# Normalised activations ahead of the first FFN part and the second input projection; convolution taps read from PSUM

## The chip, the cores and the metric

The kernel runs on one core of a Trainium2 chip. The time is device microseconds of one execution. TensorE (PE) multiplies, VectorE (DVE), ScalarE (ACT) and GpSimd (POOL) do element-wise work, SyncE (SP) issues the DMAs.

## The reference

One inference step of a one-layer hybrid decoder: 1024 prompt tokens and 8 sample tokens, model width 1024, FFN width 2816, all float32.

```python
h = rmsnorm(x, norm_mix)                       # x * rsqrt(mean(x*x)+eps) * g
proj = h @ w_in
...                                            # four recurrent mixers: S5, mLSTM, GLA, RWKV-7
x = x + mix @ w_out
h2 = rmsnorm(x, norm_ffn)
ug, uv = split(h2 @ ffn_w_up)                  # gate and value, 2816 columns each
padded = concatenate([ffn_buf, ug])
conv = ffn_conv_b
for j in range(3): conv = conv + ffn_conv_w[j] * padded[:, j:j+T]
x = x + (gelu(conv) * uv) @ ffn_w_down
y = rmsnorm(x, norm_final)
```

## The kernel before

Activations lie with features on the partitions and tokens along the free axis. The tokens are worked on in two segments: 512 prompt tokens, and 520 (the other 512 and the 8 sample tokens). The program is: input projection of segment 0 (`win(0)`), a list of mixer steps (`SEQ0`), input projection of segment 1 (`win(1)`), output projection and FFN of segment 0 (the "first FFN part"), a second list of mixer steps (`SEQ1`: gla, mlstm, rwkv and s5 on the later tokens, then the decode steps of the sample tokens), then output projection and FFN of segment 1 (the "last FFN part"). A list scheduler writes the order of each engine from priorities: weight loads ('S') come first; projections, FFN and mixers are interleaved; the matmuls of `mm3` ('G') have the lowest priority and fill what the mixers leave of PE.

Each float32 product is made of three fp32r matmuls (`mm3`, L1129 to L1131): high part of the weight by high and low part of the activation, low part of the weight by high part of the activation. `load_w` fetches a weight tile (512 KB), casts it on ScalarE (L1111) and forms the low part on GpSimd (L1112, four pieces). `split_gain` (L1181, L1182) multiplies an activation by the norm's gain and splits it, on ScalarE and VectorE. The eight pieces of a segment are the tiles h0 to h7.

The factor rsqrt(mean(x*x)+eps) depends only on the token. It is applied after the matmul. `Ms` collects the squares (L1153, L1154), and `rstd` adds them over the partitions with a matmul by ones (L1161) and makes the factor with Ln and Exp on ScalarE (L1165, L1166). `w_in_fm` multiplies by it when it takes a result out of PSUM (L1204); `w_in_tm`, whose results have tokens on the partitions, uses a copy of the factor with tokens on the partitions that `tokens` makes (L1173 to L1176). The factor of segment 1 (`x_rstd`, k.r1) is computed among the mixer steps of `SEQ0`.

The FFN runs over 22 blocks j of 128 columns. For each block of the first part: 24 matmuls of 512 columns give the gate in a PSUM tile g, 24 more the value. VectorE takes the gate out with the factor (L1302) and the value too (L1309), makes the first tap with bias (L1311) and adds the two others (L1314, L1315), each from the gate in SBUF. GpSimd sets the two columns ahead of the gate to zero (L1312), keeps the last two for the next segment in `halo` (L1319) and multiplies the convolution by the value (L1327). `gelu_gate` (L124 to L126, and L119 to L121 in `sigmoid_`) makes gelu's gate; L1329 multiplies, and `split_act` (L1120, L1121) splits the result into a tile p0 to p4. After every fourth block `down` multiplies four of them by the down weights, and L1290 adds to the residual x2 (tiles xa0 to xa7 for segment 0). PSUM has three tiles g for all this until the last FFN part, which has five more.

The mixers' own PE work is of many small matmuls between VectorE steps. In `rwkv`, L242 and L243 are 31 dependent pairs of VectorE instructions (a triangular solve), L253 the matmuls behind them, and L277 to L297 a chain over four chunks of 64 tokens.

Of the kernel before, what the change touches and what calls it, by code (L numbers as in the profile page):

```python
# [1178 lines left out]
def split_gain(k,N,i,x,gname):  # L1179
# [2 lines left out]
    k.nc.vector.scalar_tensor_tensor(out=h[:,1,0:N],in0=x,scalar=g,in1=h[:,0,0:N].bitcast(F32),op0=ALU.mult,op1=ALU.subtract)  # L1182
    return h

def x_rstd(k,c0,c1):
    N=c1-c0; m=Ms(k,N,1,"mc",1)
# [4 lines left out]
    m.tokens()
    return m

def w_in_fm(k,hr,seg,idx,w=None,tag=None):
# [8 lines left out]
    for (a,b),p in zip(chunks(N),ps):
        nc.vector.scalar_tensor_tensor(out=e[:,a:b],in0=p[:,0:b-a],scalar=sc,in1=r[:,a:b],op0=ALU.mult,op1=ALU.mult)  # L1204
# [69 lines left out]

def ffn(k,c0,c1,x2,rs,last=False,then=None):
    nc=k.nc; V=nc.vector; A=nc.scalar; GP=nc.gpsimd; N=c1-c0
    lastseg=c1==1032; NP=N-8 if lastseg else N
    hs=[split_gain(k,N,i,x2[i][:,0:N],'nffn') for i in range(8)]; ms=None if last else Ms(k,N)
    ch=chunks(N); o=2*last
    hid={}  # L1280
    def down(n):
        ph=[hid.pop(j) for j in range(max(4*n-o,0),min(4*n-o+4,22))]; end=n==5; nm=8//len(ph)
        wd=lambda i,tags=None: load_w(k,(k.wdn,k.wdl)[last][max(4*n-o,0)+i].rearrange("p (m k c)->p m k c",m=nm,c=128),tags)
        if last and end: return ffn_last(k,c0,x2,ch,ph,[wd(0),wd(1),wd(2,("h0","h1")),wd(3,("h2","h3"))])
        for m in range(8):
            if m%nm==0: w=wd(m//nm)
            for a,b in ch:
                p=gps(k)
                mm3(k,p[:,0:b-a],(w[0][:,m%nm],w[1][:,m%nm]),ph,a,b)
                V.tensor_tensor(out=x2[m][:,a:b],in0=x2[m][:,a:b],in1=p[:,0:b-a],op=ALU.add)  # L1290
            if end: ms.add(x2[m][:,0:N])

    for j in range(22):
        wg=load_w(k,k.wup[j,0]); wv=load_w(k,k.wup[j,1])
        g=k.tp.tile([128,HW+2],F32,tag="t",name="t",bufs=k.tb); acc=tt(k)
        pv=[]; pg=[]
        for a,b in ch:
            p=gps(k); pg.append(p)
            mm3(k,p[:,0:b-a],wg,hs,a,b)
        r=rs.rstd()  # L1300
        for (a,b),p in zip(ch,pg):
            V.tensor_tensor(out=g[:,2+a:2+b],in0=p[:,0:b-a],in1=r[:,a:b],op=ALU.mult)  # L1302
        for a,b in ch:
            q=gps(k)
            mm3(k,q[:,0:b-a],wv,hs,a,b)
            pv.append(q)
        if not last:
            qr=tt(k)
            for (a,b),q in zip(ch,pv): V.tensor_tensor(out=qr[:,a:b],in0=q[:,0:b-a],in1=r[:,a:b],op=ALU.mult)  # L1309
        if last: A.activation(out=acc[:,0:N],in_=g[:,2:2+N],func=AF.Identity,scale=v1(k,'cw2',j),bias=v1(k,'cb',j))  # L1310
        else: V.tensor_scalar(out=acc[:,0:N],in0=g[:,2:2+N],scalar1=v1(k,'cw2',j),scalar2=v1(k,'cb',j),op0=ALU.mult,op1=ALU.add)  # L1311
# [2 lines left out]
        V.scalar_tensor_tensor(out=acc[:,0:NP],in0=g[:,1:1+NP],scalar=v1(k,'cw1',j),in1=acc[:,0:NP],op0=ALU.mult,op1=ALU.add)  # L1314
        V.scalar_tensor_tensor(out=acc[:,0:NP],in0=g[:,0:NP],scalar=v1(k,'cw0',j),in1=acc[:,0:NP],op0=ALU.mult,op1=ALU.add)  # L1315
        if lastseg:
            V.tensor_tensor(out=acc[:,NP:N],in0=acc[:,NP:N],in1=k.sdec[:,j],op=ALU.add)
            GP.tensor_copy(k.fcd[:,j],g[:,2+NP:2+N])
        GP.tensor_copy(k.halo[:,j],g[:,NP:NP+2])  # L1319
        if last:  # L1320
            A.activation(out=acc[:,0:N],in_=acc[:,0:N],func=AF.Gelu_apprx_tanh)
            if j==21: k.tc.keep_in_program_order(A.preload_act_table_set("natural_log_exp_and_others"))
            GP.tensor_tensor(out=acc[:,0:N],in0=acc[:,0:N],in1=r[:,0:N],op=ALU.mult)
            for (a,b),q in zip(ch,pv):
                V.tensor_tensor(out=acc[:,a:b],in0=acc[:,a:b],in1=q[:,0:b-a],op=ALU.mult)
        else:
            GP.tensor_tensor(out=qr[:,0:N],in0=acc[:,0:N],in1=qr[:,0:N],op=ALU.mult)  # L1327
            gelu_gate(k,g[:,2:2+N],acc[:,0:N])
            V.tensor_tensor(out=acc[:,0:N],in0=qr[:,0:N],in1=g[:,2:2+N],op=ALU.mult)  # L1329
# [212 lines left out]
```

## Time and profile before

| | us |
|---|---|
| runs shown, median of 3 | 1537.26 (1534.96 to 1538.24) |
| the profiled execution, its own time | 1529.54 |
| its span, first to last instruction | 1527.7 |
| PE busy | 1426.4 (93%) |
| PE weight loads | 1244.7 (81%) |
| VectorE busy | 1055.3 (69%) |
| ScalarE busy | 631.8 (41%) |
| GpSimd busy | 926.5 (61%) |

The page also cuts the span into 40 slices of 38 us. A digit is the busy share in tenths; PEclk is the clock that PE was granted, in tenths of full speed.

```profile
PE   8699999997998989999789999989999999999997
DVE  8998856888588968897896868586436434343444
PEclk9889999998999999999989999999999999999999
```

The last FFN part fills the last ten slices, where PE has no gap and VectorE is a third to a half busy. A matmul is pipelined: its own time (0.40 us for 512 columns) is longer than the distance between two of them (0.23 us), so PE's busy time is read as the union of intervals.

### The profile page before, as it was taken

To read this page: it belongs to the slowest core of one execution; us is meant where nothing else is said; L and a number is where in the kernel's file an instruction comes from. 1 tells how busy PE (TensorE), PEld (TensorE's weight loads), DVE (VectorE), ACT (ScalarE), POOL (GpSimd) and SP (SyncE) were. 2 spreads that over 40 slices of the span, in tenths; PEclk is the share of its full clock that TensorE was granted. 3 is DMA by queue.
4 is the path that set the end of the run, shared out by engine and by line. 5 is a ranking of instruction groups with operands and counts; after the bars stand their busy time and mean duration, and the time that the engine had idled before them with its cause. 6 is when DMAs were issued, how large, how long until landed. Compare 5 with 4: busy or idle time off the path is not lost.

```text
span 1527.7 us, 26826 instructions
## 1 busy us (share of the span) xinstructions
PE 1426.4 (93%) x10123; PEld 1244.7 (81%) x10123; DVE 1055.3 (69%) x2096; ACT 631.8 (41%) x1007; POOL 926.5 (61%) x1182
## 2 busy tenths in 40 slices
PE   8699999997998989999789999989999999999997
PEld 7577779877898767767567777767999999999997
DVE  8998856888588968897896868586436434343444
ACT  6135354534445454463435524334442323232323
POOL 8555354544345455556655567596877758576764
PEclk9889999998999999999989999999999999999999
DMA  6554348434243523532323343324334323223332
GB/s 222 161 161 160 96 150 238 143 93 91 85 145 118 170 84 97 169 111 72 90 67 95 91 149 116 97 89 160 118 105 138 98 85 96 96 87 95 93 91 84
DMA packets 110806, 179.80 MB, mean 118 GB/s; under 512 B 33556, under 2 KB 67732, under 8 KB 110676
## 3 DMA queue, kind: packets, MB, share of 16 engines
q1 hardware_dynamic: 110676, 178.08, 38.2%
q8 instruction: 80, 1.31, 0.4%
q14 instruction: 50, 0.41, 0.1%
HBM read 148.10 MB, written 28.41 MB: 116 GB/s over the span
## 4 chain that ended last, share of the span: by engine, by line
PE 42%; DVE 15%; POOL 3%; ACT 2%; issue 2%; DMA 2%; DVEq 0%; SPq 0%; ACTq 0%; POOLq 0%
PE g L1129 13%; PE g L1130 13%; PE g L1131 13%; POOL wl L1112 2%; DVE r_rs L243 2%; DVE r L242 1%; DVE t L1315 1%; DVE t L1314 1%; DVE t L125 1%; DVE p L1121 1%; DVE xa L1290 0%; DVE t L1372 0%; DVE t L1329 0%; DVE t L126 0%; DMA r<-DB 0%
## 5 line engine op out<-in xcount | busy, mean ns | idle before, releaser
L1112 POOL TENSOR_TENSOR wl<-wr,wh 128x256 fp32r<-128x256 f32 x708 | 593.2, 869 | 242.3 <-ACT wh L1111 220.7
L1131 PE MATMUL g<-h,wl 128*128 128x260 f32 (+1 forms) x1536 | 492.2, 321 | 3.6 <-POOL wl L1112 3.5
L1129 PE MATMUL g<-h,wh 128*128 128x260 f32 (+1 forms) x1536 | 491.9, 321 | 3.0 <-DVE t L1204 1.8
L1130 PE MATMUL g<-h,wh 128*128 128x260 f32 (+1 forms) x1536 | 492.3, 321 | 1.6 <-DVE h L1182 1.4
L1131 PEld LDWEIGHTS g<-h,wl 128*128 128x128 f32 x1536 | 290.1, 189 | 28.5 <-POOL wl L1112 5.9
L1130 PEld LDWEIGHTS g<-h,wh 128*128 128x128 f32 x1536 | 289.5, 189 | 26.9 <-DVE h L1182 2.9
L1129 PEld LDWEIGHTS g<-h,wh 128*128 128x128 f32 x1536 | 289.5, 189 | 25.8 <-issue 2.0
L1111 ACT CAST wh<-wr 128x1024 fp32r<-128x1024 f32 x177 | 185.0, 1045 | 298.8 <-PE g L1130 166.4
L1129 PE MATMUL g<-p,wh 128*128 128x260 f32 (+1 forms) x496 | 162.8, 330 | 17.8 <-DVE xa L1290 6.9
L1130 PE MATMUL g<-p,wh 128*128 128x260 f32 (+1 forms) x496 | 163.0, 329 | 1.4 <-DVE p L1121 1.3
L1131 PE MATMUL g<-p,wl 128*128 128x260 f32 (+1 forms) x496 | 162.8, 329 | 1.3 <-POOL wl L1112 1.3
L1129 PEld LDWEIGHTS g<-p,wh 128*128 128x128 f32 x496 | 94.8, 192 | 28.2 <-DVE xa L1290 7.4
L1131 PEld LDWEIGHTS g<-p,wl 128*128 128x128 f32 x496 | 94.9, 192 | 10.1 <-POOL wl L1112 2.0
L1130 PEld LDWEIGHTS g<-p,wh 128*128 128x128 f32 x496 | 94.6, 191 | 10.3 <-DVE p L1121 2.7
L1112 POOL TENSOR_TENSOR p<-p,p 128x256 fp32r<-128x256 f32 x76 | 62.7, 856 | 54.7 <-ACT p L1111 42.1
L1302 DVE TENSOR_TENSOR t<-g,r 128x260 f32<-128x260 f32 (+1 forms) x66 | 33.6, 511 | 63.6 <-PE g L1131 57.6
L1290 DVE TENSOR_TENSOR xb<-xb,g 128x260 f32<-128x260 f32 x80 | 33.6, 424 | 59.2 <-PE g L1131 59.1
L1314 DVE SCALAR_TENSOR_TENSOR t<-t,vec 128x512 f32<-128x512 f32 x44 | 41.2, 937 | 25.9 <-ACT t L1310 25.3
L1121 DVE TENSOR_TENSOR p<-t,p 128x512 fp32r<-128x512 f32 (+1 forms) x44 | 40.8, 928 | 18.6 <-ACT p L1120 18.4
L1130 PE MATMUL g<-h,p 128*128 128x260 f32 (+1 forms) x144 | 50.8, 353 | 2.1 <-DVE h L1121 2.1
L1129 PE MATMUL g<-h,p 128*128 128x260 f32 (+1 forms) x144 | 51.6, 358 | 0.0
L1131 PE MATMUL g<-h,p 128*128 128x260 f32 (+1 forms) x144 | 50.4, 350 | 0.0
(722 smaller groups left out, 2744.4 us busy)
## 6 DMA issues: line engine op xcount, KB each, us to landing
wr<-in_wup_dram SPq DMA_DIRECT2D x88, 512.0 KB
wr<-in_wfm_dram SPq DMA_DIRECT2D x27, 512.0 KB
wr<-in_wdn_dram SPq DMA_DIRECT2D x22, 512.0 KB
wr<-in_wdl_dram SPq DMA_DIRECT2D x22, 512.0 KB
wr<-in_wout_dram SPq DMA_DIRECT2D x13, 512.0 KB
p<-in_wfm_dram SPq DMA_DIRECT2D x11, 512.0 KB
t<-in_xT_dram SPq DMA_DIRECT2D x16, 260.0 KB
b4c<-B8Td SPq DMA_DIRECT2D x6, 512.0 KB
```

The source lines that it names most:

```text
L125: k.nc.vector.scalar_tensor_tensor(out=t,in0=t,scalar=1.0,in1=x,op0=ALU.add,op1=ALU.mult)
L242: V.tensor_tensor(out=tv,in0=bc(Ls[:,jj+1:32,jj:jj+1],[128,n,m]),in1=bc(X[:,jj:jj+1,0:m],[128,n,m]),op=ALU.mult)
L243: V.tensor_tensor(out=X[:,jj+1:32,0:m],in0=X[:,jj+1:32,0:m],in1=tv,op=ALU.subtract)
L1111: nc.scalar.copy(h[:,0:n],r[:,0:n])
L1112: for c in range(0,n,256): nc.gpsimd.tensor_tensor(out=l[:,c:c+256],in0=r[:,c:c+256],in1=h[:,c:c+256].bitcast(F32),op=ALU.subtract)
L1121: k.nc.vector.tensor_tensor(out=h[:,1,0:N],in0=src,in1=h[:,0,0:N].bitcast(F32),op=ALU.subtract)
L1129: T.matmul(out,wh[:,i],a,start=i==0,stop=False)
L1130: T.matmul(out,wh[:,i],b,start=False,stop=False)
L1131: T.matmul(out,wl[:,i],a,start=False,stop=i==n-1)
L1290: V.tensor_tensor(out=x2[m][:,a:b],in0=x2[m][:,a:b],in1=p[:,0:b-a],op=ALU.add)
L1302: V.tensor_tensor(out=g[:,2+a:2+b],in0=p[:,0:b-a],in1=r[:,a:b],op=ALU.mult)
L1314: V.scalar_tensor_tensor(out=acc[:,0:NP],in0=g[:,1:1+NP],scalar=v1(k,'cw1',j),in1=acc[:,0:NP],op0=ALU.mult,op1=ALU.add)
```

## The change

In `win(1)` and in the first FFN part the factor is now applied to the activations ahead of the split: the new `split_norm` multiplies each of the eight tiles by it on GpSimd and hands the product to `split_gain`. The factor after the matmul goes in these two places. The evictions of `w_in_fm` in `win(1)` become ScalarE activations; `w_in_tm` multiplies by 1.0; `w_in_g` drops its product; `x_rstd` no longer makes the copy with tokens on the partitions. `win(0)` and the last FFN part keep the factor where it was.

In the first FFN part (`gate_first`) the gate stays in PSUM: ScalarE makes the first tap with bias from it, the two other taps read it there and write from column 1 and column 2 on, so that no columns need to be set to zero. ScalarE copies the last two columns into `halo` and takes the value out of PSUM. The last FFN part (`gate_last`) has the same instructions as before.

```diff
+def split_norm(k,N,i,x,r,gname):
+    t=tt(k)[:,0:N]; k.nc.gpsimd.tensor_tensor(out=t,in0=x,in1=r[:,0:N],op=ALU.mult)
+    return split_gain(k,N,i,t,gname)
+
 def x_rstd(k,c0,c1):
...
-    m.tokens()
+    m.rstd()
     return m
 def w_in_fm(k,hr,seg,idx,w=None,tag=None):
...
-    r=r.rstd()
+    if r is not None: r=r.rstd()
     for (a,b),p in zip(chunks(N),ps):
-        nc.vector.scalar_tensor_tensor(out=e[:,a:b],in0=p[:,0:b-a],scalar=sc,in1=r[:,a:b],op0=ALU.mult,op1=ALU.mult)
+        if r is None: nc.scalar.activation(out=e[:,a:b],in_=p[:,0:b-a],func=AF.Identity,scale=sc)
+        else: nc.vector.scalar_tensor_tensor(out=e[:,a:b],in0=p[:,0:b-a],scalar=sc,in1=r[:,a:b],op0=ALU.mult,op1=ALU.mult)
...
 def ffn(k,c0,c1,x2,rs,last=False,then=None):
...
-    hs=[split_gain(k,N,i,x2[i][:,0:N],'nffn') for i in range(8)]; ms=None if last else Ms(k,N)
+    hs=[split_gain(k,N,i,x2[i][:,0:N],'nffn') if last else split_norm(k,N,i,x2[i][:,0:N],rs.rstd(),'nffn') for i in range(8)]; ms=None if last else Ms(k,N)
...
+    def gate_first(j,wg,wv):
+        acc=tt(k); t=tt(k); qr=tt(k); p=up(wg)[0]
+        A.activation(out=acc[:,0:N],in_=p[:,0:N],func=AF.Identity,scale=v1(k,'cw2',j),bias=v1(k,'cb',j))
+        for o,n in ((1,'cw1'),(2,'cw0')): V.scalar_tensor_tensor(out=acc[:,o:N],in0=p[:,0:N-o],scalar=v1(k,n,j),in1=acc[:,o:N],op0=ALU.mult,op1=ALU.add)
+        A.copy(k.halo[:,j],p[:,N-2:N])
+        q=up(wv)[0]
+        A.copy(qr[:,0:N],q[:,0:N])
+        GP.tensor_tensor(out=qr[:,0:N],in0=acc[:,0:N],in1=qr[:,0:N],op=ALU.mult)
+        gelu_gate(k,t[:,0:N],acc[:,0:N])
+        V.tensor_tensor(out=acc[:,0:N],in0=qr[:,0:N],in1=t[:,0:N],op=ALU.mult)
+        return acc
...
-        r=rs.rstd()
-        for (a,b),p in zip(ch,pg):
-            V.tensor_tensor(out=g[:,2+a:2+b],in0=p[:,0:b-a],in1=r[:,a:b],op=ALU.mult)
...
-        if not last:
-            qr=tt(k)
-            for (a,b),q in zip(ch,pv): V.tensor_tensor(out=qr[:,a:b],in0=q[:,0:b-a],in1=r[:,a:b],op=ALU.mult)
-        if last: A.activation(out=acc[:,0:N],in_=g[:,2:2+N],func=AF.Identity,scale=v1(k,'cw2',j),bias=v1(k,'cb',j))
-        else: V.tensor_scalar(out=acc[:,0:N],in0=g[:,2:2+N],scalar1=v1(k,'cw2',j),scalar2=v1(k,'cb',j),op0=ALU.mult,op1=ALU.add)
-        if c0==0: GP.memset(g[:,0:2],0.0)
-        else: GP.tensor_copy(g[:,0:2],k.halo[:,j])
-        V.scalar_tensor_tensor(out=acc[:,0:NP],in0=g[:,1:1+NP],scalar=v1(k,'cw1',j),in1=acc[:,0:NP],op0=ALU.mult,op1=ALU.add)
-        V.scalar_tensor_tensor(out=acc[:,0:NP],in0=g[:,0:NP],scalar=v1(k,'cw0',j),in1=acc[:,0:NP],op0=ALU.mult,op1=ALU.add)
...
     for j in range(22):
         wg=load_w(k,k.wup[j,0]); wv=load_w(k,k.wup[j,1])
+        acc=(gate_last if last else gate_first)(j,wg,wv)
...
     def setup():
...
-                w=[]; hr=[split_gain(k,c1-c0,i,load_x(k,i,c0,c1),'nmix') for i in range(8)],k.r1
+                w=[]; hr=[split_norm(k,c1-c0,i,load_x(k,i,c0,c1),k.r1.rstd(),'nmix') for i in range(8)],None
```

The scheduler writes a new order for all engines from about the middle of `SEQ0` up to the second output projection. Three places follow. In rows of the order, a name is the output tile, then the inputs behind the arrow.

PE at the start of the first FFN part, before: h_5414 is the output projection's last activation tile, h_5735 and on are the FFN's first ones, and L277 is a matmul of the rwkv chain.

```order
L1130 MATMUL g<-h_5414,wh 128x512
L1131 MATMUL g<-h_5414,wl 128x512
L1129 MATMUL g<-h_5735,wh 128x512
L1130 MATMUL g<-h_5735,wh 128x512
L1131 MATMUL g<-h_5735,wl 128x512
L1129 MATMUL g<-h_5738,wh 128x512
L1130 MATMUL g<-h_5738,wh 128x512
```

The same place on PE now: h_5417 is the output projection's last tile, and the first FFN matmul (h_5745) stands 42 rows behind it.

```order
L1130 MATMUL g<-h_5417,wh 128x512
L1131 MATMUL g<-h_5417,wl 128x512
L289 MATMUL ma<-r_KB,r_8930 128x128 x2
L296 MATMUL ma<-r_KR,r_S 64x64
L297 MATMUL ma<-r_rc,r_KB 64x64
```

Rows between them are the rwkv chain (L277 to L297), the matmul by ones (L1161) and mLSTM's small matmuls; before, L1161 stood behind the first block's 24 gate matmuls. What moved: the mixers' small matmuls came forward into the place where FFN matmuls stood.

GpSimd at the same place, before: L1154 adds squares, L1112 forms low parts of weights, L1312 is the memset ahead of a gate.

```order
L1112 TENSOR_TENSOR wl<-wr,wh 128x256 x4
L1154 TENSOR_TENSOR s<-s,t 128x512
L441 TENSOR_TENSOR b2a<-b2a,b2e 128x512
L1154 TENSOR_TENSOR s<-s,t 128x512
L1312 MEMSET t 128x2
L1112 TENSOR_TENSOR wl<-wr,wh 128x256 x4
L1154 TENSOR_TENSOR s<-s,t 128x512
L1112 TENSOR_TENSOR wl<-wr,wh 128x256 x4
```

GpSimd now, from the last addition of squares on:

```order
L1112 TENSOR_TENSOR wl<-wr,wh 128x256 x4
L1154 TENSOR_TENSOR s<-s,t 128x512
L1187 TENSOR_TENSOR t<-xa_5371,r 128x512
L1187 TENSOR_TENSOR t<-xa_5372,r 128x512
L1187 TENSOR_TENSOR t<-xa_5373,r 128x512
L1187 TENSOR_TENSOR t<-xa_5374,r 128x512
L1187 TENSOR_TENSOR t<-xa_5375,r 128x512
L1187 TENSOR_TENSOR t<-xa_5376,r 128x512
L1187 TENSOR_TENSOR t<-xa_5377,r 128x512
L1187 TENSOR_TENSOR t<-xa_5378,r 128x512
L1112 TENSOR_TENSOR wl<-wr,wh 128x256 x4
```

The eight products of `split_norm` stand in a row between the last addition and the next low part of a weight.

More of the change, by code (lines that the diff above doesn't have):

```diff
@@ L1231, in w_in_tm @@
         e=tt(k)
-        for u in range(2): A.activation(out=e[:,u*256:u*256+256],in_=ps[i//2][:,u*256:u*256+256],func=AF.Identity,scale=r.rT[:,i+u:i+u+1])
+        for u in range(2): A.activation(out=e[:,u*256:u*256+256],in_=ps[i//2][:,u*256:u*256+256],func=AF.Identity,scale=r.rT[:,i+u:i+u+1] if r else 1.0)
         nc.sync.dma_start(out=dst[c0+i*128:c0+i*128+256].rearrange("(u p) f->p u f",p=128),in_=e[:,0:512].rearrange("p (u f)->p u f",u=2))
@@ L1237, in w_in_tm @@
         V.tensor_tensor(out=e,in0=e,in1=q[32:32+m,0:256],op=ALU.add)
-        V.tensor_scalar(out=e,in0=e,scalar1=r.rT[0:m,n:n+1],scalar2=None,op0=ALU.mult)
         nc.sync.dma_start(out=dst[c0+n*128:c1],in_=e)
@@ L1253, in w_in_g @@
         nc.vector.tensor_tensor(out=e[:,a:b],in0=e[:,a:b],in1=p[32:64,0:b-a],op=ALU.add)
-    nc.gpsimd.tensor_tensor(out=e[:,0:N],in0=e[:,0:N],in1=r.rstd()[0:32,0:N],op=ALU.mult)
+    if r: nc.gpsimd.tensor_tensor(out=e[:,0:N],in0=e[:,0:N],in1=r.rstd()[0:32,0:N],op=ALU.mult)
     nc.sync.dma_start(out=k.rowD[:,c0:c1],in_=e[:,0:N])
@@ L1276, in ffn @@
     nc=k.nc; V=nc.vector; A=nc.scalar; GP=nc.gpsimd; N=c1-c0
-    lastseg=c1==1032; NP=N-8 if lastseg else N
-    hs=[split_gain(k,N,i,x2[i][:,0:N],'nffn') for i in range(8)]; ms=None if last else Ms(k,N)
+    NP=N-8
+    hs=[split_gain(k,N,i,x2[i][:,0:N],'nffn') if last else split_norm(k,N,i,x2[i][:,0:N],rs.rstd(),'nffn') for i in range(8)]; ms=None if last else Ms(k,N)
     ch=chunks(N); o=2*last
@@ L1291, in down, with up @@
             if end: ms.add(x2[m][:,0:N])
+    def up(w):
+        ps=[]
+        for a,b in ch:
+            p=gps(k); ps.append(p)
+            mm3(k,p[:,0:b-a],w,hs,a,b)
+        return ps
+    def gate_first(j,wg,wv):
[9 more added lines that the diff above has]
+        return acc
@@ new lines, in gate_last @@
+    def gate_last(j,wg,wv):
+        g=k.tp.tile([128,HW+2],F32,tag="t",name="t",bufs=k.tb); acc=tt(k)
+        pg=up(wg); r=rs.rstd()
+        for (a,b),p in zip(ch,pg): V.tensor_tensor(out=g[:,2+a:2+b],in0=p[:,0:b-a],in1=r[:,a:b],op=ALU.mult)
+        pv=up(wv)
+        A.activation(out=acc[:,0:N],in_=g[:,2:2+N],func=AF.Identity,scale=v1(k,'cw2',j),bias=v1(k,'cb',j))
+        GP.tensor_copy(g[:,0:2],k.halo[:,j])
+        V.scalar_tensor_tensor(out=acc[:,0:NP],in0=g[:,1:1+NP],scalar=v1(k,'cw1',j),in1=acc[:,0:NP],op0=ALU.mult,op1=ALU.add)
+        V.scalar_tensor_tensor(out=acc[:,0:NP],in0=g[:,0:NP],scalar=v1(k,'cw0',j),in1=acc[:,0:NP],op0=ALU.mult,op1=ALU.add)
+        V.tensor_tensor(out=acc[:,NP:N],in0=acc[:,NP:N],in1=k.sdec[:,j],op=ALU.add)
+        GP.tensor_copy(k.fcd[:,j],g[:,2+NP:2+N])
+        GP.tensor_copy(k.halo[:,j],g[:,NP:NP+2])
+        A.activation(out=acc[:,0:N],in_=acc[:,0:N],func=AF.Gelu_apprx_tanh)
+        if j==21: k.tc.keep_in_program_order(A.preload_act_table_set("natural_log_exp_and_others"))
+        GP.tensor_tensor(out=acc[:,0:N],in0=acc[:,0:N],in1=r[:,0:N],op=ALU.mult)
+        for (a,b),q in zip(ch,pv): V.tensor_tensor(out=acc[:,a:b],in0=acc[:,a:b],in1=q[:,0:b-a],op=ALU.mult)
+        return acc
@@ L1293, in ffn @@
     for j in range(22):
         wg=load_w(k,k.wup[j,0]); wv=load_w(k,k.wup[j,1])
[L1295 to L1299, printed above, removed]
-        r=rs.rstd()
-        for (a,b),p in zip(ch,pg):
[L1302 to L1306, printed above, removed]
@@ L1315, in ffn @@
[L1315 to L1329, printed above, removed]
+        acc=(gate_last if last else gate_first)(j,wg,wv)
```

## The prediction

> **What bounds the kernel now.** I read the stages first, then what TensorE (PE) waits for, then the engine behind those waits. The table by stage has, per row, the window in us, its length, busy time and instruction count of PE, PEld, DVE, ACT and POOL, then the granted PE clock, DMA share and GB/s.
>
> ```profile
> 240.00:563.00 323.00, 294.83 (x2495) 261.08 (x2495) 255.29 (x533) 149.89 (x263) 159.32 (x211) 0.97 0.45 129
> 563.00:806.00 243.00, 224.23 (x1319) 170.12 (x1318) 208.04 (x375) 115.61 (x185) 140.06 (x171) 0.97 0.33 101
> 806.00:1050.00 244.00, 232.14 (x1335) 183.64 (x1332) 179.88 (x296) 102.22 (x181) 170.36 (x193) 0.99 0.34 104
> 1050.00:1140.00 90.00, 87.96 (x593) 80.49 (x592) 39.23 (x58) 41.29 (x58) 67.46 (x82) 1.00 0.44 141
> ```
>
> 240 to 563 is the second input projection beside mixers; 563 to 1140 is the first FFN part, first beside mixers (the last rwkv block solve ends at 806), then beside the decode steps, then beside the last output projection. PE is the bound everywhere: 92 to 98% busy. The change removes no matmul of weight, so only PE's idle time and its slow clock can be won: idle 28.2, 18.8, 11.9 and 2.0 us in the four rows; clock loss, as length times (1 - clock), 9.7, 7.3, 2.4 and 0. From about 1140 on all engines keep their old order.
>
> PE's waits from 560 to 1110 (total, times, longest):
>
> ```profile
> PE g L1129 <- DVE xa L1290: 6.9, 2, 4.1
> PE g L1131 <- POOL wl L1112: 4.3, 3, 2.1
> PE g L1129 <- DVE t L1302: 4.3, 2, 2.8
> PE mb L335 <- DVE r_rs L243: 2.7, 1, 2.7
> PE g L1129 <- ACT p L1120: 2.5, 1, 2.5
> PE g L1129 <- ACT wh L1111: 2.3, 1, 2.3
> ```
>
> 13.9 us in these rows end with VectorE, 4.3 with GpSimd, 4.8 with ScalarE. Two finer windows (same columns) and PE's order of time (start, us) show how:
>
> ```profile
> 740.00:760.00 20.00, 14.85 (x60) 10.58 (x59) 19.69 (x35) 10.93 (x19) 14.94 (x17) 0.97 0.28 92
> 760.00:780.00 20.00, 14.94 (x74) 10.84 (x73) 19.81 (x32) 6.04 (x9) 11.47 (x15) 0.78 0.16 54
> ```
> ```profile
> 781.57 0.50 PE L1129 MATMUL g<-p,wh 128*128 128x512 f32 x1 [4.10 <-DVE xa L1290]
> ...
> 784.30 0.63 PE L1131 MATMUL g<-p,wl 128*128 128x512 f32 x1
> 784.73 0.63 PE L1129 MATMUL g<-p,wh 128*128 128x512 f32 x1
> ...
> 786.48 0.39 PE L1131 MATMUL g<-p,wl 128*128 128x512 f32 x1
> 786.70 0.39 PE L1129 MATMUL g<-p,wh 128*128 128x512 f32 x1
> ```
>
> VectorE is full (19.7 and 19.8 of 20), PE waits for a PSUM buffer behind its queue, and after the 4.1 us wait the matmuls start 0.43 apart instead of 0.23. So a VectorE backlog costs twice, and its load is what the change cuts.
>
> **The change, part by part.**
>
> *VectorE in the first FFN part.* Its ten groups there, 22 iterations (busy us, mean ns | idle before):
>
> ```profile
> L1290 DVE TENSOR_TENSOR xa<-xa,g 128x512 f32<-128x512 f32 x48 | 32.4, 679 | 17.8 <-PE g L1131 17.8
> L125 DVE SCALAR_TENSOR_TENSOR t<-t 128x512 f32<-128x512 f32 x22 | 23.8, 1082 | 5.7 <-ACT t L124 5.6
> L1314 DVE SCALAR_TENSOR_TENSOR t<-t,vec 128x512 f32<-128x512 f32 x22 | 21.5, 978 | 0.6
> L1315 DVE SCALAR_TENSOR_TENSOR t<-t,vec 128x512 f32<-128x512 f32 x22 | 21.5, 975 | 0.3
> L1121 DVE TENSOR_TENSOR p<-t,p 128x512 fp32r<-128x512 f32 x22 | 20.5, 932 | 5.4 <-ACT p L1120 5.2
> L1311 DVE TENSOR_SCALAR t<-t,vec 128x512 f32<-128x512 f32 x22 | 17.4, 792 | 0.0
> L1329 DVE TENSOR_TENSOR t<-t 128x512 f32<-128x512 f32 x22 | 17.3, 784 | 17.5 <-ACT t L121 13.5 <-ACT d_xm L119 2.1 <-ACT d_s L879 1.0
> L1302 DVE TENSOR_TENSOR t<-g,r 128x512 f32<-128x512 f32 x22 | 15.1, 684 | 5.8 <-PE g L1131 4.8 <-ACT r L1166 1.0
> L1309 DVE TENSOR_TENSOR t<-g,r 128x512 f32<-128x512 f32 x22 | 15.0, 682 | 8.2 <-PE g L1131 8.1
> L126 DVE TENSOR_SCALAR t<-t 128x512 f32<-128x512 f32 x22 | 14.3, 649 | 0.4
> ```
>
> L1302, L1309 and L1311 go: 15.1 + 15.0 + 17.4 = 47.5 us. The two taps (L1314, L1315) read the gate from PSUM. The nearest row is the projection's eviction, the same operation with one input in PSUM (ns, min/median/max):
>
> ```profile
> L1204 DVE SCALAR_TENSOR_TENSOR t<-mb,r x2: 678/681/684, 46.1 to 56.0; 128x512 f32<-128x512 f32 x2
> ```
>
> At 681 instead of 976 the 44 taps save 44 x 0.295 = 13.0 us; if they kept 976 they would save nothing. Sum 60.5 us, or 16% of the 388 us that VectorE is busy from 563 to 1050; per iteration 198.8/22 = 9.04 us becomes 6.29.
>
> [...]
>
> *What that is worth.* Not 60 us: only what hangs on it of 32.7 us of idle time and 9.7 us of clock loss from 563 to 1140. Ends: 0 and -42. Rows with 13.9 of 32.7 us of waiting end with VectorE, 43%, so some 18 us are in reach; I take two thirds of them, 12 us, because a queue's backlog shrinks faster than its load. 2 us more come from GpSimd, whose 22 memsets and 22 halo copies go: POOL no longer stops in its in-order queue for L1302 ahead of a weight residue, a part of the 4.3 us in the second row of waits. Split evenly: **-7 us** up to 806 (of 18.8 + 7.3) and **-7 us** after it (of 11.9 + 2.4 + 2.0).
>
> *ScalarE gains* the first tap, the value copy and the halo copy per iteration. Nearest rows, both from PSUM:
>
> ```profile
> L1165 ACT ACTIVATE r<-g,eps x6: 478/478/688, 581.9 to 1518.1; 128x260 f32<-128x260 f32 x4, 128x512 f32<-128x512 f32 x2
> L431 ACT COPY b2c<-mb x4: 586/586/587, 199.9 to 823.1; 128x512 f32<-128x512 f32 x4
> ```
>
> 0.69 + 0.59 + about 0.2 (two columns, between 0 and 0.59) = 1.5 us, 22 times 33 us. ACT is busy 217.8 of 487 us from 563 to 1050, so it goes to some 51%; I take 0. The gate's PSUM buffer, freed before by one 0.68 us eviction, is now held through 0.69 + 2 x 0.68 + 0.2 = 2.3 us and whatever lies ahead in two queues. There are three buffers, and a group of 24 matmuls takes 24 x 0.23 = 5.5 us, so the next two groups hide up to about 11 us. Without that cover, the extra 1.6 us x 22 would be 35 us. I take 0.
>
> *Start of the first FFN part.* Before, normalising came after the matmul, so FFN matmuls follow the output projection's last ones directly. Now PE waits for the whole chain:
>
> ```profile
> 563.29 0.69 DVE L1270 TENSOR_TENSOR xa<-t,g 128x512 f32<-128x512 f32 x1 [1.85 <-PE g L1131]
> 564.62 0.61 ACT L1153 ACTIVATE t<-xa 128x512 f32<-128x512 f32 x1
> 580.46 1.13 PE L1161 MATMUL g<-s,ones 128*128 128x512 f32 x2
> 585.20 0.63 ACT L1166 ACTIVATE r<-r 128x512 f32<-128x512 f32 x1
> ```
> ```profile
> L1154 POOL TENSOR_TENSOR s<-s,t x21: 1273/1299/1454, 525.3 to 1134.7; 128x512 f32<-128x512 f32 x14, 128x520 f32<-128x520 f32 x7
> L1181 ACT ACTIVATE h<-xa,vec x8: 708/713/726, 564.0 to 573.5; 128x512 fp32r<-128x512 f32 x8
> L1182 DVE SCALAR_TENSOR_TENSOR h<-xa,vec,h x8: 732/745/1437, 564.8 to 575.3; 128x512 fp32r<-128x512 f32 x8
> ```
>
> Addition 0.69, square 0.61, sum 1.30, ones 1.13, Ln 0.69, Exp 0.63: 5.05 us. Then eight GpSimd products at 1.30 (the L1154 form) end 10.4 us later, gain and residue of the last 0.71 + 0.75: 16.9 us, against 11.0 us for iteration 0's 48 matmuls, which used to run in this time. 5.9 us later, plus up to 2 us of slow clock and some queueing; the mixers' small matmuls that the new order puts into the gap are work brought forward, up to 5 us. Ends +1 and +12; I take **+6 us**.
>
> [...]
>
> *Second input projection.* 38 VectorE evictions go to ScalarE, eight GpSimd products come (10.4 us) ahead of the gains, and the token table with its small matmuls goes.
>
> ```profile
> L1204 DVE SCALAR_TENSOR_TENSOR t<-g,r 128x260 f32<-128x260 f32 x38 | 15.7, 420 | 10.3 <-PE g L1131 10.0
> ```
> ```profile
> PE mb L367 <- POOL wl L1112: 6.5, 1, 6.5
> PE ma L253 <- ACT r_KB L245: 3.4, 1, 3.4
> ```
>
> VectorE loses 15.7 us of 255, ScalarE gains 38 x 0.478 = 18 on 150 of 323. The longest PE waits there hang on POOL and ACT, which get more work. The statistics are ready long before, so only the pace of GpSimd (1.30 against 0.75 per tile) is late. Ends -15 and +12; I take -2 for relief and +2 for the start: **0**.
>
> **Sum:** -7 - 7 + 6 + 0 = **-8 us**. The profiled execution took 1529.5 us (span 1527.7) and would take 1521.5; the shown median of three is 1537.3, so 1529.
>
> **The rivals.**
>
> *The mixers do not keep up (slower).* Between the last output-projection matmul and the last rwkv solve the order has 649 filler matmuls of 512 columns before, 396 now: 253 x 0.23 = 58 us less cover, so this 243 us stretch must shrink to 185. VectorE loses there 649/72 x 9.04 - 396/72 x 6.29 = 46.9 us, which leaves 161 of 185 us, 87% against 86% before. If the chain only gains those 47 us, PE idles 11 us more: +11 - 7 + 6 = +10, 1547 (the start's 6 us come ahead of the stretch). It decides from where idle and clock loss of that stretch pass 27 us (26.1 now). The like utilisation speaks for it, the gaps of up to 4.1 us that single VectorE bursts cause against it. A PSUM slot that comes late (above) ends on the same side, near 1545.
>
> *The stretch keeps its idle share (no change):* 0 - 7 + 6 = -1, 1536.
>
> *Backlogs vanish:* -18 - 13 + 2 = -29, 1508, if the full windows at 740 to 800 empty and the start is filled by mixers. That the taps do not get cheaper (13 us less relief) moves the sum by only about +3.
>
> **How the numbers follow.** Forecast 0.42, large gain 0.14, no change 0.16, slower 0.28 (mixers 0.20, PSUM or ScalarE 0.08). A measurement of this kernel tells about 0.2%, 3 us, from no change: faster 0.56, same 0.16, slower 0.28. Predicted 1529; the range 1510 to 1548 leaves out about 0.07 below and 0.12 above. The likeliest case alone spans 1519 to 1534.
>
> **What would show it.** VectorE rows gone at L1302, L1309 and L1311 and taps near 0.68 us; from the start of the first FFN part to the start of the last one less than 42 us of idle time and clock loss; one PE gap of 5 to 8 us after the output projection with 0.43 us matmuls behind it; PE waits on VectorE below 12 us. Wrong, if new waits of PE for ScalarE's first tap or value copy (L1306, L1310 of the changed kernel) appear, or if the solve stretch idles over 27 us.

## The result, and the profile after

| | median us | ratio to before, 95% interval |
|---|---|---|
| predicted | 1529 (against 1537.26 shown) | 0.995 |
| measured, 4 runs of each | 1523.70 (before 1536.11) | 0.9920, 0.9896 to 0.9944 |
| measured again, 8 runs (before 31 runs) | 1524.59 (before 1535.82) | 0.9924, 0.9899 to 0.9949 |

The change takes 12 us off; 8 were forecast. The new kernel's stages, in the same windows as before (length, busy time and count of PE, PEld, DVE, ACT, POOL, then clock, DMA share, GB/s):

```profile
240.00:563.00 323.00, 303.89 (x2560) 269.16 (x2560) 232.32 (x495) 162.04 (x303) 159.81 (x214) 0.96 0.44 127
563.00:806.00 243.00, 223.76 (x1412) 171.37 (x1410) 195.50 (x364) 129.32 (x218) 137.11 (x157) 0.95 0.32 98
806.00:1050.00 244.00, 234.61 (x1194) 186.07 (x1194) 139.84 (x247) 113.40 (x207) 162.57 (x175) 0.98 0.39 119
1050.00:1140.00 90.00, 87.99 (x599) 80.94 (x598) 34.41 (x53) 41.91 (x61) 67.64 (x80) 1.00 0.34 108
```

PE's idle time falls from 28.2 to 19.1 us in the first row, the second input projection, for which nothing was forecast. All its waits for VectorE there, added up, fall from 15.5 to 9.2 us. In the second it is 19.2 (18.8 before) and in the third 9.4 (11.9 before), although VectorE's busy time falls by 12.5 and by 40 us there. The clock is a little lower in three rows (0.96, 0.95 and 0.98; before 0.97, 0.97 and 0.99). The stretch in which VectorE was full before is no longer full (same columns), though the new order has partly other work there:

```profile
740.00:760.00 20.00, 19.72 (x134) 14.64 (x132) 17.10 (x15) 12.36 (x22) 19.56 (x21) 1.00 0.35 117
760.00:780.00 20.00, 16.79 (x130) 13.28 (x131) 16.68 (x33) 10.88 (x18) 8.41 (x10) 0.83 0.18 53
```

What PE waits for from 560 to 1110 (us in total, times, longest):

```profile
PE ma L289 <- DVE r_KB L286: 4.2, 2, 3.3
PE g L1131 <- POOL wl L1112: 4.0, 3, 2.2
PE g L1130 <- DVE h L1182: 3.0, 3, 2.4
PE g L1129 <- DVE xa L1295: 2.5, 1, 2.5
PE mb L335 <- DVE b4d L115: 2.4, 1, 2.4
```

The waits for a PSUM buffer behind VectorE's queue have shrunk: 6.9 us for L1290 are 2.5 for L1295 (the same instruction), and the 4.3 us for L1302 are gone with it. In their place stand waits of the mixers' own chain (L289) and the new start (L1182). Added up over all rows, from the output projection's last addition to the last FFN part, PE waits 18.9 to 20.8 us for VectorE in four profiles of before, and 22.8 and 21.4 us in two of the changed kernel: this sum did not fall. The wait for GpSimd's weight residue is what it was, 4.0 against 4.3.

The rows of the moved work, first VectorE's taps, then ScalarE's three (busy us, mean ns, idle before):

```profile
L1307 DVE SCALAR_TENSOR_TENSOR t<-g,vec,t 128x511 f32<-128x511 f32 x22 | 16.4, 747 | 27.2 <-ACT t L1306 27.1
L1307 DVE SCALAR_TENSOR_TENSOR t<-g,vec,t 128x510 f32<-128x510 f32 x22 | 16.3, 739 | 0.1
```
```profile
L1306 ACT ACTIVATE t<-g,vec 128x512 f32<-128x512 f32 x22 | 17.0, 772 | 0.1
L1310 ACT COPY t<-g 128x512 f32<-128x512 f32 x22 | 12.7, 577 | 0.0
L1308 ACT COPY halo<-g 128x2 f32<-128x2 f32 x22 | 3.5, 160 | 29.2 <-DVE t L1307 29.1
```

VectorE now waits 27 us for ScalarE's first tap and ScalarE 29 us for the taps, but neither is among PE's longer waits, and all of PE's waits for ScalarE from that addition to the last FFN part are 1.8 us (5.8 before): these are waits off the path.

Four events cut both kernels into stretches with the same PE work, up to a shift of the fillers: the output projection's last addition, the last rwkv solve (L253), and the ones of the last FFN part. After, then before, in order of time:

```profile
571.22 0.69 DVE L1275 TENSOR_TENSOR xa<-t,g 128x512 f32<-128x512 f32 x1
...
732.69 1.91 PE L253 MATMUL ma<-r_KB,r_rc 32*32 32x32 f32 x32 [0.91 <-ACT r_KB L245]
...
1135.31 1.15 PE L1161 MATMUL g<-s,ones 128*128 128x260 f32 x4 [1.77 <-POOL s L1154]
```
```profile
571.77 0.68 DVE L1270 TENSOR_TENSOR xa<-t,g 128x512 f32<-128x512 f32 x1
...
805.62 1.19 PE L253 MATMUL ma<-r_KB,r_rc 32*32 32x32 f32 x32
...
1136.05 1.14 PE L1161 MATMUL g<-s,ones 128*128 128x260 f32 x4 [1.76 <-POOL s L1154]
```

The last solve starts 73 us earlier, with 58 us less of fillers (the 512-column matmuls of projection and FFN) ahead of it: the mixers did keep up. But the last FFN part starts at almost the same time. In this pair of profiles (spans 1524.5 and 1527.7) only 3 of the 12 us can be seen, so more profiles and parts of the change were run.

### The profile page after: what moved, and what is told of

The parts are those of the page before. It is cut to its first block, busy times and chain, and to the rows that moved or that the text cites. A ratio compares the mean times of both kernels' runs of the same rounds, so it can differ in the third digit from the quotient of the medians.

```text
span 1524.5 us, 26739 instructions
## 1 busy us (share of the span) xinstructions
PE 1431.6 (94%) x10113; PEld 1250.3 (82%) x10113; DVE 967.5 (63%) x1987; ACT 668.9 (44%) x1111; POOL 918.7 (60%) x1153
## 4 chain that ended last, share of the span: by engine, by line
PE 45%; DVE 13%; POOL 2%; issue 2%; ACT 2%; DMA 2%; SPq 0%; DVEq 0%; POOLq 0%; ACTq 0%
PE g L1129 14%; PE g L1130 14%; PE g L1131 14%; POOL wl L1112 1%; DVE r L242 1%; DVE r_rs L243 1%; DMA r_rc<-rcD 1%; DVE b4c L515 1%; DVE t L125 1%; DVE h L1182 0%; DVE t L1378 0%; PE mb L395 0%; DVE t L1307 0%; DMA b4b<-MD 0%; DVE yo L1359 0%
## 5 line engine op out<-in xcount | busy, mean ns | idle before, releaser
L1112 POOL TENSOR_TENSOR wl<-wr,wh 128x256 fp32r<-128x256 f32 x708 | 587.1, 861 | 305.9 <-ACT wh L1111 283.5
L1112 POOL TENSOR_TENSOR p<-p,p 128x256 fp32r<-128x256 f32 x76 | 61.7, 841 | 51.3 <-ACT p L1111 48.8
L1295 DVE TENSOR_TENSOR xb<-xb,g 128x260 f32<-128x260 f32 x80 | 33.6, 424 | 59.2 <-PE g L1131 59.2
L1295 DVE TENSOR_TENSOR xa<-xa,g 128x512 f32<-128x512 f32 x48 | 32.8, 683 | 34.6 <-PE g L1131 34.5
L1318 DVE TENSOR_TENSOR t<-g,r 128x260 f32<-128x260 f32 x44 | 18.6, 424 | 56.2 <-PE g L1131 51.3
L1307 DVE SCALAR_TENSOR_TENSOR t<-g,vec,t 128x511 f32<-128x511 f32 (+1 forms) x44 | 32.7, 743 | 27.3 <-ACT t L1306 27.1
L1129 PE MATMUL g<-h,p 128*128 128x260 f32 (+1 forms) x144 | 49.6, 344 | 0.0
L1130 PE MATMUL g<-h,p 128*128 128x260 f32 (+1 forms) x144 | 49.3, 342 | 0.0
L1131 PE MATMUL g<-h,p 128*128 128x260 f32 (+1 forms) x144 | 49.3, 342 | 0.0
```

The lines of the kernel that those rows point to most:

```text
L1112: for c in range(0,n,256): nc.gpsimd.tensor_tensor(out=l[:,c:c+256],in0=r[:,c:c+256],in1=h[:,c:c+256].bitcast(F32),op=ALU.subtract)
L1129: T.matmul(out,wh[:,i],a,start=i==0,stop=False)
L1130: T.matmul(out,wh[:,i],b,start=False,stop=False)
L1131: T.matmul(out,wl[:,i],a,start=False,stop=i==n-1)
L1307: for o,n in ((1,'cw1'),(2,'cw0')): V.scalar_tensor_tensor(out=acc[:,o:N],in0=p[:,0:N-o],scalar=v1(k,n,j),in1=acc[:,o:N],op0=ALU.mult,op1= ...
L1318: for (a,b),p in zip(ch,pg): V.tensor_tensor(out=g[:,2+a:2+b],in0=p[:,0:b-a],in1=r[:,a:b],op=ALU.mult)
```

## The experiments

Kernels of one group ran on one chip beside the kernel before: the first four, the next four, the last four. Ratios are to before, with 95% intervals.

**1 and 2. Both kernels again.** No edit.

> The changed kernel once more, for a tight ratio and a second profile. All theories expect the ratio measured first, 0.992 (about -12 us, 0.990 to 0.994). Theory (VectorE relief pays, the start costs): in the second profile the sum of idle time and clock loss from the start of the first FFN part to the start of the last one is under 42 us, and the first profile, whose 32 us + 16 us are no better than before, was a run with an unluckily throttled clock. Rival (the first FFN part won nothing, the gain is elsewhere): that sum is again about 48 us, and the gain stands ahead of the first FFN part or behind it.

> The kernel before, for a second profile. Its first profiled execution, 1529.5 us at a granted clock of 0.975, is shorter than all four of its timed runs (1534 to 1538). Theory: a second profile has a lower clock (0.970 or less) and more idle time and clock loss between 563 and 1140 us (over 45 us, against 42.4 in the first), so that part of the 12 us is there. Rival (the first profile is typical): the same stages within 2 us each, and a time near 1530.

The changed kernel: 1524.59 us, ratio 0.9924 (0.9899 to 0.9949). The kernel before: 1533.0 over 8 runs, ratio to its other runs 0.9992 (0.9960 to 1.0024); its second profile has a span of 1528.6 at a clock of 0.973 and the same long waits as the first, each within 1 us. So the lower clock that the theory expected did not show, and its rival, that the first profile is typical of this place, held. In the changed kernel's second profile idle time and clock loss between the output projection's last addition and the last FFN part are 28.6 + 17.1 us, in the first 30.6 + 16.9 (summed over windows of 12 us); before they were 32.6 + 8.5 and 31.6 + 11.9. So the forecast's mark "under 42 us" is missed both times, and the rival's reading holds: little is gained inside that stretch (its length is 564.8 us on average before and 562.9 after).

**3 and 4. Each part alone.** The projection alone:

```diff
-    m.tokens()
+    m.rstd()
...
-                w=[]; hr=[split_gain(k,c1-c0,i,load_x(k,i,c0,c1),'nmix') for i in range(8)],k.r1
+                w=[]; hr=[split_norm(k,c1-c0,i,load_x(k,i,c0,c1),k.r1.rstd(),'nmix') for i in range(8)],None
```

with the ScalarE evictions of `w_in_fm` that belong to it; the FFN alone is the changed kernel without these lines.

> The kernel before with only the second input projection changed (normalised activations, ScalarE evictions, no token table). Theory, as the prediction had it: 0 us (ratio 0.998 to 1.002), 2 us of relief against 2 us of a slower start. Rival: this part carries half or more of the gain, -6 us or more (ratio 0.996 or less), because VectorE loses 16 us there and fewer small matmuls run.

> The kernel before with only the first FFN part changed (normalised activations, taps that read PSUM, value by ScalarE). Theory, as the prediction had it: the whole gain, -8 to -12 us (ratio 0.992 to 0.995), and the sum of this one and of the run with the input projection alone is that of the whole change. Rival (the gain is the input projection's): -3 us or less of gain (ratio 0.998 or more).

Projection alone: 1532.51 us, ratio 0.9979 (0.9960 to 0.9999), some -3 us. FFN alone: 1528.94, ratio 0.9962 (0.9941 to 0.9982), some -6 us. Both lie between what the theory and its rival expected: the FFN does not carry the whole gain. The sum of the two, -9, and the whole, -12, agree within their intervals. The projection's interval runs from almost nothing to half of the gain.

The clock loss (span times 1 minus granted clock) blurs these times. Without it the mean spans are 1489.4 us for before, 1483.5 for the projection alone, 1481.7 for the FFN alone and 1475.6 for both, each to about 1 us: -5.9, -7.7 and -13.8. By this measure the parts add up, and the projection carries some two fifths.

**5. Normalised activations in the FFN without the relief.** The changed start stays; VectorE's ten groups and GpSimd's memset and halo copy come back.

```diff
-        A.activation(out=acc[:,0:N],in_=p[:,0:N],func=AF.Identity,scale=v1(k,'cw2',j),bias=v1(k,'cb',j))
+        V.tensor_copy(g[:,2:2+N],p[:,0:N])
...
-        A.copy(qr[:,0:N],q[:,0:N])
+        V.tensor_copy(qr[:,0:N],q[:,0:N])
+        V.tensor_scalar(out=acc[:,0:N],in0=g[:,2:2+N],scalar1=v1(k,'cw2',j),scalar2=v1(k,'cb',j),op0=ALU.mult,op1=ALU.add)
+        GP.memset(g[:,0:2],0.0)
...
+        GP.tensor_copy(k.halo[:,j],g[:,N:N+2])
```

> The first FFN part takes normalised activations, but VectorE still evicts gate and value (as plain copies) and forms the first tap from SBUF, so its ten groups an iteration stay and only the later start remains. Against the run with the first FFN part alone (ratio 0.9962, -6 us). Theory (relief -14, start +6): about +6 us over before (ratio 1.002 to 1.007), 12 us over that run. Rival (the gain does not come from VectorE's load but from the new order and from normalising early): within 3 us of that run (ratio 0.994 to 0.998).

1560.88 us, ratio 1.0161 (1.0130 to 1.0193): +25 us over before and 32 over the run with the FFN alone. The theory has the sign, but both of its terms are far too small. Of the 26 us between the mean spans (1559.3, and 1533.6 of before beside it) 17 are clock loss (62.6 against 46.0). Its three events, in its profile (the longest of its executions; the second row is the last 24 of the 32 matmuls):

```profile
579.87 0.69 DVE L1276 TENSOR_TENSOR xa<-t,g 128x512 f32<-128x512 f32 x1 [0.36 <-PE g L1131]
...
755.81 0.92 PE L253 MATMUL ma<-r_KB,r_rc 32*32 32x32 f32 x24
...
1171.78 1.29 PE L1161 MATMUL g<-s,ones 128*128 128x260 f32 x4 [1.77 <-POOL s L1154]
```

Up to the last solve it takes 175.9 us, with 242 fillers fewer than before (56 us): no worse than the 233.8 of before's first profile. The loss stands behind the solve, 416.0 us against 330.4 + 56; idle time and clock loss there are 29.6 + 10.2 us, in before's first profile 13.9 + 1.7. PE's waits there:

```profile
PE g L1129 <- DVE xa L1296: 10.0, 6, 4.8
PE g L1131 <- POOL wl L1112: 8.5, 9, 3.8
PE mc L952 <- DVE d_g L941: 4.2, 1, 4.2
```

The fillers that the new order moves behind the solve bring their VectorE work along. VectorE is busy for 67% of that stretch, against 66% in before, so it is not the bound on average; what PE waits for are its bursts, and GpSimd's residues. That the moved fillers cause them is argued: no run has the new form in the old order.

**6. The start without its wait.** The first FFN part's products take the factor of the input projection, which is long ready. Its own factor, with two matmuls of ones, Ln and Exp, is left out, so the result is not the reference's:

```diff
-    hs=[split_gain(k,N,i,x2[i][:,0:N],'nffn') if last else split_norm(k,N,i,x2[i][:,0:N],rs.rstd(),'nffn') for i in range(8)]; ms=None if last else Ms(k,N)
+    hs=[split_gain(k,N,i,x2[i][:,0:N],'nffn') if last else split_norm(k,N,i,x2[i][:,0:N],k.r1.rstd(),'nffn') for i in range(8)]; ms=None if last else Ms(k,N)
```

> The changed kernel, but the first FFN part is multiplied by the factor of the second input projection, which is ready long before; its own statistics (two matmuls of ones, Ln, Exp) are left out, so the values are not the reference's. The start then waits for one product, gain and residue only. Theory (the start costs 6 us): 5 to 8 us under the changed kernel (ratio to before 0.987 to 0.989), and the wait of PE for L1182 after the output projection gone. Rival (mixers fill the start, it costs nothing): within 2 us of the changed kernel (0.991 to 0.994).

1518.12 us, ratio 0.9888 (0.9859 to 0.9918), 6.5 us under the changed kernel's median (5.5 by the ratios). Of its timeline the first products on GpSimd, PE's longest wait and the first row of the steady FFN matmuls, and the first and last of these in the changed kernel:

```profile
572.74 5.69 POOL L1187 TENSOR_TENSOR t<-xa,r 128x512 f32<-128x512 f32 x4
...
581.19 0.66 PE L277 MATMUL ma<-r_S,r_KR 128*64 128x128 f32 x2 [3.54 <-DVE r_S L292]
...
583.06 0.80 PE L1130 MATMUL g<-h,wh 128*128 128x512 f32 x1
```
```profile
581.33 6.27 POOL L1187 TENSOR_TENSOR t<-xa,r 128x512 f32<-128x512 f32 x5 [5.83 <-ACT r L1166]
...
589.52 0.51 PE L1130 MATMUL g<-h,wh 128*128 128x512 f32 x1 [2.43 <-DVE h L1182]
```

The matmuls flow 6.5 us earlier, 1.5 us of which stand ahead of the start (the output projection's last addition comes at 569.7 and 571.2). PE's wait for L1182 is gone, as the theory expected, and the time agrees with the forecast 6 us. But the run does not take the idle time out of the start: a wait for the rwkv chain (L292) stands there now, and in the 25 us behind that addition PE idles 6.9 us, in the changed kernel 6.7. Its order moves 201 fillers behind the solve, not 253. So what waiting for the factor costs in all is confirmed in size; where the time goes is not shown.

**7. The projection with its evictions on VectorE.**

```diff
-        if r is None: nc.scalar.activation(out=e[:,a:b],in_=p[:,0:b-a],func=AF.Identity,scale=sc)
+        if r is None: nc.vector.tensor_scalar(out=e[:,a:b],in0=p[:,0:b-a],scalar1=sc,scalar2=None,op0=ALU.mult)
```

> The second input projection alone changed, as in the run with 0.9979 (-3 us), but its evictions stay on VectorE (one input in place of two). Theory (that gain is VectorE's relief of 16 us there): the gain goes, ratio 0.999 to 1.002. Rival (it is the normalising ahead of the matmuls and the order that comes with it): the ratio stays at 0.996 to 0.998.

1535.97 us, ratio 1.0005 (0.9984 to 1.0027): no gain is left, as the theory has it, though the interval overlaps with that of the projection with ScalarE's evictions. The output projection's last addition shows where; this kernel, then the one with the evictions on ScalarE:

```profile
587.39 0.69 DVE L1275 TENSOR_TENSOR xa<-t,g 128x512 f32<-128x512 f32 x1
```
```profile
565.85 0.69 DVE L1275 TENSOR_TENSOR xa<-t,g 128x512 f32<-128x512 f32 x1
```

It comes 21.5 us later, while the 38 evictions are 15.8 us of VectorE time (420 ns each). Most of this comes back later, since this order also puts 26 of the mixers' VectorE instructions (some 15 us) more ahead of that addition. The 21.5 us are relief and order together. So are the times: these runs lose 56.5 us to the clock on average, before beside them 46.0, and without the clock loss this kernel is 9 us shorter than before. The end result fits the relief but does not separate it from the order that comes with it.

**8. Four of the eight products on VectorE.**

```diff
-    t=tt(k)[:,0:N]; k.nc.gpsimd.tensor_tensor(out=t,in0=x,in1=r[:,0:N],op=ALU.mult)
+    t=tt(k)[:,0:N]; (k.nc.vector if gname=='nffn' and i%2==0 else k.nc.gpsimd).tensor_tensor(out=t,in0=x,in1=r[:,0:N],op=ALU.mult)
```

> The changed kernel, with four of the eight products at the start of the first FFN part on VectorE in place of GpSimd. Theory (the start hangs on GpSimd's eight products of 1.3 us): the products take some 5 us instead of 10, and the time falls by 2 to 4 us against the changed kernel (ratio to before 0.989 to 0.991). Rival (VectorE's own mixer work stands ahead of the gains' residues and sets the start): no gain or up to 3 us slower (0.992 to 0.995).

1524.23 us, ratio 0.9928 (0.9901 to 0.9955): no gain. VectorE's part of the start, and PE's first row of the steady FFN matmuls:

```profile
581.55 3.50 DVE L1187 TENSOR_TENSOR t<-xa,r 128x512 f32<-128x512 f32 x3
...
586.03 1.41 DVE L1182 SCALAR_TENSOR_TENSOR h<-t,vec,h 128x512 fp32r<-128x512 f32 x2
587.36 2.41 DVE L515 SCALAR_TENSOR_TENSOR b4c<-b4b,m_tok,cf 128x128 f32<-128x128 f32 x5
589.69 0.74 DVE L1182 SCALAR_TENSOR_TENSOR h<-t,vec,h 128x512 fp32r<-128x512 f32 x1
```
```profile
591.71 0.80 PE L1130 MATMUL g<-h,wh 128*128 128x512 f32 x1
```

The products are ready earlier (the last one ends at 593.5 us, in the changed kernel at 595.1), but their residues (L1182) stand behind an mLSTM burst (L515) in VectorE's queue, and the matmuls flow 2.2 us later than in the changed kernel.

**9. The run without relief, GpSimd freed of the gate.** The memset goes, the taps skip the first columns, and ScalarE copies the halo.

```diff
-        GP.memset(g[:,0:2],0.0)
-        V.scalar_tensor_tensor(out=acc[:,0:N],in0=g[:,1:1+N],scalar=v1(k,'cw1',j),in1=acc[:,0:N],op0=ALU.mult,op1=ALU.add)
+        V.scalar_tensor_tensor(out=acc[:,1:N],in0=g[:,2:1+N],scalar=v1(k,'cw1',j),in1=acc[:,1:N],op0=ALU.mult,op1=ALU.add)
...
-        GP.tensor_copy(k.halo[:,j],g[:,N:N+2])
+        A.copy(k.halo[:,j],g[:,N:N+2])
```

> The run without relief (ratio 1.0161, +25 us) with one thing changed: GpSimd no longer touches the gate (the memsets go, the halo copies go to ScalarE, the taps skip the first columns). VectorE keeps its ten groups. Theory (the 31 us between that run and the one with the first FFN part alone are VectorE's load): less than 8 us comes back (ratio 1.010 to 1.017). Rival (GpSimd, stopped in its queue by the halo copy behind VectorE's eviction, holds up the weight residues): most of it comes back, 15 us or more (ratio 1.006 or less), and PE's wait for GpSimd's residue falls from 9.8 us to about 4.

1555.18 us, ratio 1.0132 (1.0098 to 1.0165): of the 32 us some 6 come back. What GpSimd waited for in the kernel before, from 571 to 1136, shows why this was worth asking:

```profile
POOL wl L1112 <- ACT wh L1111: 90.1, 45, 6.3
POOL halo L1319 <- DVE t L1302: 33.3, 12, 7.3
POOL t L1327 <- DVE t L1315: 21.8, 11, 4.4
```

GpSimd stood 33 us behind VectorE's eviction for a copy of two columns. With the copy moved, PE's wait for the residue falls from 8.5 to 3.1 us in the last stretch, as the rival said, yet the time falls by 6 us, not 15, and PE's idle time behind the solve is the same in both profiles (29.6 and 30.1 us). So a fifth of the relief goes with GpSimd's queue, and the rest with VectorE's groups.

**10. A quarter of the relief given back.** FFN alone, the value evicted by VectorE:

```diff
-        A.copy(qr[:,0:N],q[:,0:N])
+        V.tensor_copy(qr[:,0:N],q[:,0:N])
```

> The first FFN part alone changed (ratio 0.9962, -6 us), but the value is evicted by VectorE: 22 x 0.68 = 15 us of VectorE's relief given back of some 58, and ScalarE loses 22 x 0.58 = 13 us. Theory (the time follows VectorE's load, 31 us of time for 58 us): +8 us, ratio 1.000 to 1.003. Rival (only GpSimd's queue counts, or VectorE's load has a threshold that this stays under): within 2 us of the run with the value on ScalarE, 0.995 to 0.998.

1532.91 us, ratio 0.9985 (0.9959 to 1.0011), 4 us over the FFN alone: between the two expectations. 15 us of VectorE's load cost 4 us; the next step, to the run without relief, adds 43 us of load and costs some 22 beside GpSimd's 6. This looks like a price per us that rises with the load, but the intervals are wide enough for a straight line too.

**11 and 12. Two more profiles of before.**

> A third profile of the kernel before. Its first two (1527.7 and 1528.6 us) lie some 6 us under the mean span of its runs, 1534. Theory: the first FFN part and the input projection have the same waits, and where the execution is longer it is longer by clock loss between 0 and 1140 us. Rival: a longer execution has other, longer waits in the first FFN part.

> A fourth profile of the kernel before, for the same question as the third.

One run each, 1533.79 and 1536.44 us, with spans of 1532.0 and 1534.6. The long waits are those of the first profile again, each within 2 us. From the output projection's last addition on, the four profiles agree within 2.2 us (955.9, 957.9, 957.3 and 955.7 us to the end of the span); that addition itself comes at 571.8, 570.7, 574.7 and 578.9. One place of the difference, in the fourth profile and then in the first (columns as above):

```profile
284.00:288.00 4.00, 2.71 (x20) 1.68 (x20) 3.88 (x11) 0.81 (x2) 1.22 (x1) 0.56 0.32 90
288.00:292.00 4.00, 4.00 (x22) 2.52 (x20) 1.51 (x4) 0.63 (x1) 0.97 (x6) 0.50 0.47 173
292.00:296.00 4.00, 4.00 (x25) 3.35 (x23) 0.43 (x1) 2.76 (x5) 0.12 (x1) 0.66 0.57 165
```
```profile
284.00:288.00 4.00, 4.00 (x38) 3.02 (x37) 2.27 (x6) 1.65 (x4) 1.96 (x7) 1.00 0.87 269
288.00:292.00 4.00, 4.00 (x30) 3.28 (x29) 2.72 (x5) 3.70 (x8) 2.33 (x3) 1.00 0.90 237
292.00:296.00 4.00, 4.00 (x35) 4.00 (x34) 4.00 (x7) 4.00 (x8) 1.26 (x2) 1.00 0.55 164
```

At much the same point of the program one execution ran some 10 us at half clock and the other none. From 0 to that addition the clock loss is 27.3, 25.6, 27.4 and 35.7 us. The theory holds for the place and the waits: executions of before differ ahead of the first FFN part, and not in its waits. By clock it holds for the fourth profile; the third is 2.9 us longer than the first up to there with the same clock loss and the same idle time, which stays open.

## Why the prediction was right, and where it was not

The stretches side by side, in us. For the third and fourth column the fillers that an order moves behind the last solve are set back at 0.23 us each (253 in the changed kernel, 250 with the FFN alone, 242 and 249 in runs 5 and 9, 201 in run 6):

| | profiles | to the output projection's last addition | to the last solve | to the last FFN part | to the end |
|---|---|---|---|---|---|
| before | 4 | 574.0 | 233.7 | 331.1 | 392.0 |
| changed | 2 | 571.2 | 218 | 345 | 390.1 |
| FFN alone (4) | 1 | 574.3 | 225 | 338 | 390.4 |
| FFN, no relief (5) | 1 | 579.9 | 232 | 360 | 392.3 |
| no relief, GpSimd freed (9) | 1 | 576.8 | 228 | 358 | 390.7 |
| changed, start ready (6) | 1 | 569.7 | 218 | 342 | 389.2 |

**VectorE's relief in the first FFN part, -14: right in sign, too small, and not where it was put.** The three groups are gone. The taps took 0.743 us on average, not 0.681, so they save 44 x 0.233 = 10 us and not 13. With one input in PSUM their rows span only 0.727 to 0.751 us, with two SBUF inputs 0.732 to 2.877 us and 0.976 on average; what lengthens the form with two SBUF inputs, no run shows. With the same normalised start, the kernel with relief is 32 us faster than the one without, 6 of them by GpSimd, for which 2 were forecast. The estimate was two thirds of the 18 us of PE's idle time and clock loss that it put down to VectorE in before; that a backlog shrinks faster than the load was an assumption. But the change also moves fillers behind the last solve, and the relief has to pay for a density that the old profile does not have: against before, PE's waits for VectorE did not fall.

**Normalising first costs its start, +6: the start is of the right size, the term is not complete.** In the 25 us behind the output projection's last addition PE idles 6.7 and 5.8 us in the two profiles of the changed kernel and loses 1.7 and 3.5 us to the clock; in before it does neither. Run 6 gives 5.5 to 6.5 us of time. Without the relief the new form costs +25, so there are some 19 us beside the start, and run 5's profile has them behind the solve. This is the step that failed: the forecast put the moved cover into a rival, asked only whether the mixers keep up to the last solve, and took the stretch behind it to gain 7 us. Measured, the changed kernel gains 16 us up to the solve and gives 14 back behind it. Little of the 16 is idle time (18.2 to 15.0 us), and of the 14 some 9 are clock loss (2.6 to 11.7 us). A part of this pair is only moved work: besides the fillers, the order puts 104 small mixer matmuls (8,192 columns) behind the solve.

That the sum came near the measured time is luck in part: the two mis-sized terms, +25 for +6 and -32 for -14, nearly cancel, -6 or -7 instead of -8, and the projection, put at 0, adds its share.

**ScalarE at 0, and the PSUM buffer held longer at 0: right.** The first tap took 0.77 us for 0.69, the copies 0.58 and 0.16 for 0.59 and 0.2, and no long wait of PE ends with L1306 or L1310. Run 10 fits this: the value on ScalarE is the faster form (1528.94 against 1532.91 us), though the intervals overlap.

**The second input projection at 0: wrong in size.** Alone it gives -3 us (0.9960 to 0.9999), or -6 without the clock loss. PE's idle time between 240 and 563 us falls by 9 us, while I allowed 2 us of relief. The longest single waits there end with GpSimd and ScalarE, and I went by these; added up, VectorE's come to 15.5 us before, GpSimd's to 7.8 and ScalarE's to 3.7.

**The signs named beforehand.** VectorE's three rows are gone, and neither sign of being wrong appeared: no new long wait for ScalarE, and the solve stretch idles 15.8 us. Four signs of being right failed: the taps near 0.68 us; less than 42 us of idle time and clock loss; one gap of 5 to 8 us at the start (PE's longest single wait there is 2.4 and 2.8 us, the idle time comes in pieces); PE's waits for VectorE below 12 us. One reading was off too: PE is 91 to 98% busy in the four rows, not 92.

**The rivals.** The mixers kept up, also without relief (232 against 233.7), so that rival's place was wrong; its mechanism, less cover for the same VectorE work, fits the loss behind the solve in run 5, though that is argued, as said there. "Keeps its idle share" describes the stretch from the last addition to the last FFN part best: 564.8 us before, 562.9 after. "Backlogs vanish" was half true at most, for the window from 740 to 760 only, in which other work stands now.

**Profiles against runs, and what stays open.** The profiles put 2.8 us of the gain ahead of the first FFN part (4.2 with the profiles of runs 3, 6 and 8 counted in), 1.9 into it and 1.9 behind it, 7 to 8 us together. The runs say 12: mean spans are 1534.0 for before (31 runs) and 1522.4 after (8 runs). The difference is clock loss, which averages 42.5 us in the four profiles of before and 44.6 in its runs, but 50.3 in the two profiles after and 46.8 in those runs. Without it the profiles fall by 14.3 us (1488.2 to 1473.9) and the runs by 13.8. Of these 14 us, 9 are idle time of PE, 6 of them ahead of the first FFN part; the rest is shorter busy time of PE, which is not explained. Nor does a run show what brings the slow clock behind the solve.
